# Mixers: longer waits in the planner for the delta rule's decay products, and the linear attention's copies and updates first in VectorE's order

## The chip, the cores and the metric

The kernel runs on one core of one Trainium2 chip. The metric is the device time of one execution in microseconds (us). TensorE multiplies matrices, VectorE and ScalarE work element by element and read the matmuls' results from PSUM, GpSimd does element-wise work in SBUF, and SyncE issues the transfers of weights.

## The reference, cut to what matters

Two transformer blocks over 512 tokens of width 1024, in float32. The first block's token mixer is what the change touches. It projects the normed input with w_in and runs four groups of heads: softmax attention with a forget gate ("fox", four heads), a gated delta rule in chunks of 64 ("gdn", four heads), and two gated linear attentions in chunks of 16 ("hg" and "gla", four heads each):

```python
# gated delta rule, per chunk of 64
decay = exp(where(causal, G[r] - G[s], -inf))
m     = where(strict, (kb @ k.T) * decay, 0)          # then solve (m + I) w = ..., (m + I) u = ...
a_qk  = where(causal, (q @ k.T) * decay, 0)
v_new = u - w @ state
o     = q_in @ state + a_qk @ v_new
state = state * a + k_out.T @ v_new
# gated linear attention, per chunk of 16
o     = q_in @ state + a_intra @ v
state = state * a + k_out.T @ v
```

The heads' outputs are normed, gated and projected with w_out. After that come a gated feed-forward with a short convolution, a block with a short-convolution mixer and a feed-forward, and a block with latent attention and a feed-forward. None of these is touched.

## The kernel before, in words

Everything is laid out with features on the 128 partitions and the 512 tokens along the free axis. A float32 product is made of three matmuls: each operand is split into a rounded part and a rest (xh and xl, wh and wl), ScalarE makes the rounded part (L111), VectorE the rest (L112). One tile of a dense product has eight steps of three matmuls each, and the weights of a whole tile are split in one ScalarE and one VectorE instruction.

In the mixers TensorE's order is the program's (`manual_schedule`), and `conduct` writes it. It is a planner with a clock of its own, `clk`, which only TensorE's work moves (`mm` and `tr` add an estimate for each matmul; a dense one of 512 columns counts 0.216). Three lanes of work, linear attention (PSUM tag lps), delta rule (gps) and fox (fps), each with two PSUM buffers, are Python generators. A generator issues some work and then yields the time that it expects the other engines to need for it; the planner takes it up again when its clock has passed that time, and fills in with steps of the dense products (w_in's tiles, then w_out's) until then. The constants are LA = 0.68 (about one ScalarE instruction), LV = 1.0 (one on VectorE), LP = 1.5 (one on GpSimd). Where the yielded time is too short, TensorE reaches an instruction whose operand or buffer isn't ready, and waits.

The order on VectorE, ScalarE and GpSimd is made when the program is built, by a scheduler with its own estimate of when each instruction becomes ready: among those ready it takes the earliest in the program, and those issued under `high_priority` before all others. On the chip each engine then runs its instructions in that order. Before the change, `high_priority` stood in the delta rule: at gy (L1138), gx (L1143), gxt (L1146), gvt (L1191) and the state gst (L1212).

`gdn(p)` runs for two pairs of heads. It transposes k and q into tokens, squares them (ScalarE), copies k's tokens to gko (ScalarE, L1062), forms the norms, and then yields 0.0. For each head j of the pair it issues the decay products (an identity matmul of a mask, shown as gps<-mixb,identb, and four of gps<-mixc,gg), and ScalarE's exponentials gmt (L1088); yields; the k·q product, weighted on VectorE into gat (L1031); yields LV; the k·k product, weighted into gmt (L1031), with gmr, u and gxt; and yields LV. After that comes the inverse by doubling, six levels with gy, gx and gxt, and the recurrence over four blocks of 128 tokens.

`la` runs three times in its lane: hg0, gla, hg1. For each of seven block sizes it issues the product of lw and lbd, four blocks of tokens wide (or two for gla), and the part of the result that belongs to this level is copied into the attention matrix lat: on ScalarE at the first level (L1366), on VectorE with `copy_predicated` under a mask at the other six (L1368). Then the next but one level's lw and lbd are made. At the end four blocks of tokens are run through, with a state lst that VectorE updates: a copy for the first block (L1406), state times decay plus product for the second and third (L1408). Outputs are normed in `finish`, which transposes them back into a PSUM buffer of the same lane and multiplies them into a gate (L1022).

Of the kernel before, what the change touches and what calls it, by code (L numbers as in the profile page):

```python
# [15 lines left out]
ALU = mybir.AluOpType  # L16
# [629 lines left out]
LA, LV, LP = 0.68, 1.0, 1.5  # L646
# [17 lines left out]
class Mix(Mla):  # L664
# [371 lines left out]
    def gdn(self, p):  # L1036
        nc = self.nc
# [16 lines left out]
        for i, y in enumerate((k, q)):  # L1054
# [4 lines left out]
                out=ss[:, 8 - 8 * i : 16 - 8 * i], in_=sq.rearrange("p (a d) -> p a d", d=64), axis=AX.X, op=ALU.add  # L1059
# [11 lines left out]
        nc.vector.tensor_tensor(out=kof, in0=kof, in1=ik, op=ALU.mult)  # L1071
        nk = self.s1(8, "gnk", 2)
        nc.vector.tensor_tensor(out=nk, in0=ss[:, 8:16], in1=rr[:, 8:16], op=ALU.mult)
        yield 0.0
        MT, MR, AT, X, XT = [], [], [], [], []
        for j in range(2):
            rows = slice(64 * j, 64 * j + 64)
            gp = self.pst()
            self.mm(c4(gp), self.identb, bc(self.negt), stop=False)
            for c in range(4):  # L1080
                col = 4 * c + 2 * p + j
                self.mm(
                    gp[:, c * 128 : c * 128 + 128], self.g[:, col : col + 1].to_broadcast([128, 128]), self.triu,
                    start=False, stop=(c == 3),
                )
            e = self.b("gmt", bufs=2)
            for c in range(4):
                nc.scalar.activation(  # L1088
                    out=e[:, c * 128 : c * 128 + 128], in_=gp[:, c * 128 : c * 128 + 128], func=ACTF.Exp,
                    bias=bias[:, 2 * c + j : 2 * c + j + 1],  # L1090
                )
            yield Y_GDN / (1 + j)
            kp = self.pst()
            for c in range(4):
                cs = slice(c * 128, c * 128 + 128)
                self.mm(kp[:, cs], k[rows, cs], q[rows, cs])
            at = self.b("gat", bufs=2)
            self.weighted(at, kp, ik, j, e)
            yield LV
            kp = self.pst()  # L1100
            for c in range(4):
                cs = slice(c * 128, c * 128 + 128)
                self.mm(kp[:, cs], k[rows, cs], k[rows, cs])
            mt = e
            self.weighted(mt, kp, ik, j, e)
            mr = self.b("gmr", F32R, bufs=2)
            nc.scalar.activation(out=mr, in_=mt, func=ACTF.Copy)
            xt = self.b("gxt", F32R, bufs=2)
            t1 = self.t(tag="s")
            nc.vector.tensor_tensor(out=c4(t1), in0=c4(mt), in1=bc(self.nm1), op=ALU.mult)  # L1110
            nc.vector.tensor_tensor(out=c4(xt), in0=c4(t1), in1=bc(self.ident), op=ALU.add)
            MT.append(mt), MR.append(mr), AT.append(at), XT.append(xt)
            yield LV
        nc.gpsimd.tensor_tensor(out=d4(ke), in0=d4(ko), in1=b64(eG), op=ALU.mult)
        nc.gpsimd.tensor_tensor(out=d4(ko), in0=d4(ko), in1=b64(h2(kof)), op=ALU.mult)
        tp = self.to_tokens(v)
# [8 lines left out]
        for lv in range(6):  # L1125
            b = 2 << lv
# [12 lines left out]
            for j in range(2):  # L1139
                yield LV  # L1140
                pp = self.mm4(XT[j], Y[j], up)
# [3 lines left out]
                with self.tc.high_priority():  # L1145
                    nc.vector.scalar_tensor_tensor(  # L1146
                        out=lo(XT[j]), in0=lo(pt), scalar=self.grow[:, lv : lv + 1], in1=lo(f1(XT[j])),
                        op0=ALU.mult, op1=ALU.add,
# [31 lines left out]
        st = None  # L1180
        yield LA
        for c in range(4):
# [3 lines left out]
            else:  # L1186
# [3 lines left out]
                with self.tc.high_priority():  # L1190
# [5 lines left out]
                    out=h64(os_[:, cs]), in0=h64(qp[:, 0:128]),  # L1196
                    in1=eG[:, c].unsqueeze(2).to_broadcast([128, 2, 64]), op=ALU.mult,
                )
                yield 0.5
            if c < 3:  # L1200
                kp = self.pst()
# [120 lines left out]
    def la(self, q, k, f, vts, nh, es, pair, gates, g, scale):  # L1322
# [30 lines left out]
        for lv, b in enumerate(LEVELS):  # L1353
            w, bd = ws[lv]
            per = 512 // (nh * 64)
            for c0 in range(0, 4, per):
                yield wait
                wait = LV
                pp = self.pst().rearrange("p (c h r) -> p c h r", c=per, h=nh)
                for c in range(per):  # L1360
                    cs = slice((c0 + c) * 128, (c0 + c) * 128 + 128)
                    self.mm(pp[:, c], w[:, cs], bd[:, c0 + c])
                for h in range(nh):
                    at = c4(AT[h])[:, c0 : c0 + per]
                    if lv == 0:
                        nc.scalar.activation(out=at[0:64, :, 64:128], in_=pp[0:64, :, h], func=ACTF.Copy)  # L1366
                    else:
                        nc.vector.copy_predicated(  # L1368
                            out=at.rearrange("p c (n j) -> p c n j", j=2 * b)[:, :, :, b:],
                            mask=self.lmask[:, lv - 1].rearrange("p (n j) -> p n j", j=b).unsqueeze(1)  # L1370
                            .to_broadcast([128, per, 64 // b, b]),
                            data=pp[:, :, h].rearrange("p c (n j) -> p c n j", j=b),
                        )
            if lv + 2 < len(LEVELS):
                ws.append(self.la_level(lv + 2, q, k, g128, g16, es, nh))
                wait = LV + LP
# [17 lines left out]
        for c in range(4):  # L1394
            cs = slice(c * 128, c * 128 + 128)
            yield LV
            if c < 3:
                kp = self.pst()
                for i in range(nh // 2):
                    self.mm(kp[:, i * 128 : i * 128 + 128], ko[:, cs], vts[i][:, cs])  # L1400
                new = self.ph.tile([128, 256], F32, tag="lst", name="lst", bufs=2)
                nc.gpsimd.memset(new, 0.0)
                for h in range(nh):
                    rs, vs = slice(h * dk, h * dk + dk), slice(h * 64, h * 64 + 64)
                    if st is None:
                        nc.vector.tensor_copy(out=new[rs, vs], in_=kp[rs, vs])  # L1406
                    else:
                        nc.vector.scalar_tensor_tensor(  # L1408
                            out=new[rs, vs], in0=st[rs, vs], scalar=ea[rs, c : c + 1],
                            in1=kp[rs, vs], op0=ALU.mult, op1=ALU.add,  # L1410
                        )
            op = self.pst()
            for i in range(nh // 2):
                ob = op[:, i * 128 : i * 128 + 128]
                if st is not None:
                    self.mm(ob, qi[:, cs], st[:, i * 128 : i * 128 + 128], stop=False)
                for j in range(2):
                    hs = slice(c * 128 + j * 64, c * 128 + j * 64 + 64)
                    self.mm(
                        ob[:, j * 64 : j * 64 + 64], AT[2 * i + j][:, cs], vts[i][:, hs],  # L1420
                        start=(c == 0), stop=(c == 0 or j == 1),
                    )
            for i in range(nh // 2):
                nc.scalar.activation(out=os_[i][:, cs], in_=op[:, i * 128 : i * 128 + 128], func=ACTF.Copy)
            if c < 3:
                st = new
# [268 lines left out]
```

## Time and profile before

| | |
|---|---|
| median of 3 runs | 1861.06 us (1860.66 to 1865.96) |
| profiled execution | 1856.94 us |
| its span | 1855.1 us, granted clock 0.994 |
| TensorE busy | 1817.0 us (98%) |
| VectorE busy | 1055.4 us (57%) |
| ScalarE busy | 737.9 us (40%) |
| GpSimd busy | 193.8 us (10%) |

The profile is of one execution. The span goes from its first to its last instruction, and some 1.8 us of the execution lie around it. Matmuls overlap, so a busy TensorE isn't one at its peak, but a hole in it is time in which it did nothing. The granted clock is 1.00 at 2.4 GHz and 0.50 at 1.2 GHz. The engines are named PE (TensorE), PEld (its weight loads), DVE (VectorE), ACT (ScalarE), POOL (GpSimd) and SP (SyncE).

### The profile page before, as it was taken

Reading aid. Unit: us, or ns where it says so; the run is one execution under the profiler, and the core shown is the slowest. Engines: PE = TensorE matmul, PEld = TensorE weight load, DVE = VectorE, ACT = ScalarE, POOL = GpSimd, SP = SyncE. Lnnn points to the kernel's source line nnn. Section 1 sums busy time; section 2 is a strip of 40 time slices with the busy share of each in tenths; the row PEclk is TensorE's granted clock in tenths of the full one; section 3 lists DMA queues with packets and bytes.
Section 4 is the critical chain, followed back from the end, with each engine's and each line's share of the span. In section 5 each row is a group of like instructions: output and inputs, shape, how many; then the busy total and the mean of one; then the engine's idle time right before and its main releaser. Section 6 shows DMA issues by size and latency. Waiting matters only on the chain.

```text
span 1855.1 us, 22054 instructions
## 1 busy us (share of the span) xinstructions
PE 1817.0 (98%) x8609; PEld 1501.1 (81%) x8609; DVE 1055.4 (57%) x1627; ACT 737.9 (40%) x1138; POOL 193.8 (10%) x225
## 2 busy tenths in 40 slices
PE   8999999999999999999999999999999999999997
PEld 6787788778888888888888888888787888888886
DVE  7885976767777633555564444333876454444323
ACT  6544535454444422322342323323577333232322
POOL 1511402210000001111200000010011200000001
PEclk9999999999999999999999999999999999999999
DMA  5111110322223233232323232333212232323332
GB/s 168 57 42 40 48 38 30 120 95 96 99 95 102 86 96 103 91 102 92 102 96 103 91 102 92 94 97 105 64 57 75 79 103 91 102 91 99 94 94 77
DMA packets 53223, 162.61 MB, mean 88 GB/s; under 512 B 6528, under 2 KB 13184, under 8 KB 53120
## 3 DMA queue, kind: packets, MB, share of 16 engines
q1 hardware_dynamic: 52992, 161.21, 27.2%
q8 instruction: 67, 1.10, 0.2%
q14 instruction: 36, 0.29, 0.1%
q10 hardware_dynamic: 128, 0.01, 0.0%
HBM read 157.78 MB, written 2.10 MB: 86 GB/s over the span
## 4 chain that ended last, share of the span: by engine, by line
PE 86%; DVE 8%; ACT 4%; issue 1%; POOL 1%; DMA 0%; SPq 0%; DVEq 0%; POOLq 0%; ACTq 0%
PE mm L125 24%; PE mm L127 24%; PE mm L126 24%; PE mm L705 6%; PE gps L705 3%; PE lps L705 2%; PE fps L705 1%; DVE lbd L1317 1%; ACT wh L111 1%; DVE wl L112 1%; DVE lat L1368 1%; PE ps L577 0%; DVE ptl L112 0%; PE ps L165 0%; DVE nm L580 0%
## 5 line engine op out<-in xcount | busy, mean ns | idle before, releaser
L111 ACT ACTIVATE wh<-raw 128x1024 fp32r<-128x1024 f32 (+3 forms) x308 | 308.6, 1003 | 765.3 <-PE mm L126 459.4
L125 PE MATMUL mm<-xh,wh 128*128 128x512 f32 x1336 | 521.8, 391 | 0.4 <-ACT xh L173 0.4
L126 PE MATMUL mm<-xl,wh 128*128 128x512 f32 x1336 | 520.7, 390 | 0.5 <-DVE xl L174 0.5
L127 PE MATMUL mm<-xh,wl 128*128 128x512 f32 x1336 | 519.9, 389 | 0.0
L112 DVE TENSOR_TENSOR wl<-raw,wh 128x1024 fp32r<-128x1024 f32 (+3 forms) x300 | 362.1, 1207 | 226.0 <-ACT wh L111 222.9
L126 PEld LDWEIGHTS mm<-xl,wh 128*128 128x128 f32 x1336 | 250.8, 188 | 54.6 <-DVE xl L174 1.4
L125 PEld LDWEIGHTS mm<-xh,wh 128*128 128x128 f32 x1336 | 250.8, 188 | 53.7 <-issue 1.0
L127 PEld LDWEIGHTS mm<-xh,wl 128*128 128x128 f32 x1336 | 250.8, 188 | 52.1 <-issue 0.2
L125 PE MATMUL mm<-hidh,wh 128*128 128x512 f32 (+1 forms) x614 | 236.7, 386 | 0.0
L127 PE MATMUL mm<-hidh,wl 128*128 128x512 f32 (+1 forms) x614 | 235.3, 384 | 0.0
L126 PE MATMUL mm<-hidl,wh 128*128 128x512 f32 (+1 forms) x614 | 233.8, 381 | 0.0
L127 PEld LDWEIGHTS mm<-hidh,wl 128*128 128x128 f32 x614 | 115.4, 188 | 24.2
L705 PE MATMUL mm<-xh,wh 128*128 128x512 f32 x291 | 127.9, 439 | 6.8 <-ACT xh L173 6.0
L126 PEld LDWEIGHTS mm<-hidl,wh 128*128 128x128 f32 x614 | 115.4, 188 | 23.6
L125 PEld LDWEIGHTS mm<-hidh,wh 128*128 128x128 f32 x614 | 115.5, 188 | 21.9 <-ACT wh L111 0.2
L705 PE MATMUL mm<-xh,wl 128*128 128x512 f32 x291 | 116.1, 399 | 0.8 <-DVE wl L112 0.8
L705 PE MATMUL mm<-xl,wh 128*128 128x512 f32 x291 | 115.9, 398 | 0.4 <-DVE xl L112 0.4
L278 DVE TENSOR_TENSOR u<-mm,rb 128x512 f32<-128x512 f32 x44 | 30.4, 691 | 140.9 <-PE mm L127 140.9
L158 POOL TENSOR_TENSOR z<-z,sq 128x512 f32<-128x512 f32 x31 | 50.3, 1624 | 557.3 <-ACT sq L156 519.6
L274 DVE TENSOR_TENSOR u<-mm,rb 128x512 f32<-128x512 f32 x44 | 30.4, 691 | 90.9 <-PE mm L127 90.8
L111 ACT ACTIVATE hidh<-s 128x512 fp32r<-128x512 f32 x66 | 41.8, 633 | 88.3 <-DVE s L255 57.5
L705 PEld LDWEIGHTS mm<-xh,wh 128*128 128x128 f32 x291 | 56.5, 194 | 19.1 <-ACT xh L173 6.7
(434 smaller groups left out, 2087.3 us busy)
## 6 DMA issues: line engine op xcount, KB each, us to landing
raw<-in_w_a_dram SPq DMA_DIRECT2D x52, 512.0 KB, 3.3
raw<-in_w_b_dram SPq DMA_DIRECT2D x52, 512.0 KB, 3.3
raw<-in_w_up_dram SPq DMA_DIRECT2D x44, 512.0 KB, 3.3
raw<-in_w_in_dram SPq DMA_DIRECT2D x28, 512.0 KB, 3.3
raw<-in_conv_w_in_dram SPq DMA_DIRECT2D x24, 512.0 KB, 3.3
raw<-in_w_down_dram SPq DMA_DIRECT2D x16, 448.0 KB, 3.3
raw<-in_w_a_dram SPq DMA_DIRECT2D x16, 448.0 KB, 3.3
raw<-in_w_b_dram SPq DMA_DIRECT2D x16, 448.0 KB, 3.3
```

Source lines behind the costliest of these rows:

```text
L111: nc.scalar.activation(out=h, in_=src, func=ACTF.Copy)
L112: (eng or nc.vector).tensor_tensor(out=l, in0=src, in1=h.bitcast(F32), op=ALU.subtract)
L125: nc.tensor.matmul(out=ps, lhsT=h, rhs=xh, start=(k == 0), stop=False)
L126: nc.tensor.matmul(out=ps, lhsT=h, rhs=xl, start=False, stop=False)
L127: nc.tensor.matmul(out=ps, lhsT=l, rhs=xh, start=False, stop=(k == kt - 1))
L158: eng.tensor_tensor(out=acc, in0=acc, in1=sq, op=ALU.add)
L274: nc.vector.tensor_tensor(out=g, in0=ps, in1=r, op=ALU.mult)
L278: nc.vector.tensor_tensor(out=g, in0=ps, in1=r, op=ALU.mult)
L705: self.nc.tensor.matmul(out=out, lhsT=lhsT, rhs=rhs, start=start, stop=stop)
L1317: nc.vector.tensor_tensor(out=bd[rows, :, h].rearrange("p c (n j) -> p c n j", j=b), in0=c4(q)[rows], in1=c4(d)[rows], op=ALU.mult)
L1368: nc.vector.copy_predicated(out=at.rearrange("p c (n j) -> p c n j", j=2 * b)[:, :, :, b:], mask=self.lmask[:, lv - 1].rearrange("p (n j) ...
```

## The change

Two yields in `gdn` are longer: the one ahead of the decay products goes from 0.0 to 2 × LA = 1.36, and the one behind the first head's k·k product from LV = 1.0 to 2.5 × LV = 2.5 (behind the second head's it stays LV). In `la`, the masked copies and the state updates are issued under `high_priority`. No instruction is added or removed.

```diff
@@ gdn @@
         nk = self.s1(8, "gnk", 2)
         nc.vector.tensor_tensor(out=nk, in0=ss[:, 8:16], in1=rr[:, 8:16], op=ALU.mult)
-        yield 0.0
+        yield 2 * LA
         MT, MR, AT, X, XT = [], [], [], [], []
...
             MT.append(mt), MR.append(mr), AT.append(at), XT.append(xt)
-            yield LV
+            yield LV if j else 2.5 * LV
         nc.gpsimd.tensor_tensor(out=d4(ke), in0=d4(ko), in1=b64(eG), op=ALU.mult)
@@ la @@
                     else:
-                        nc.vector.copy_predicated(
+                        with self.tc.high_priority():
+                            nc.vector.copy_predicated(
...
                 nc.gpsimd.memset(new, 0.0)
-                for h in range(nh):
+                with self.tc.high_priority():
+                    for h in range(nh):
...
```

## Rows read from the trace of the kernel before

**Rows 1.** Windows: busy us (x) of PE, PEld, DVE, ACT, POOL; clock; DMA share; GB/s.
```profile
40.00:405.00 365.00, 351.29 (x2012) 293.27 (x2011) 272.36 (x570) 176.13 (x344) 91.71 (x91) 0.98 0.18 57
405.00:1855.00 1450.00, 1433.58 (x6478) 1183.69 (x6477) 749.57 (x986) 536.72 (x750) 96.02 (x114) 1.00 0.29 93
```

**Rows 2.** Waits of TensorE, 40 to 405 us: total us, times, longest us.
```profile
PE lps L705 <- DVE gate L1022: 2.0, 1, 2.0
PE lps L705 <- DVE lat L1368: 1.7, 1, 1.7
PE gps L705 <- DVE gat L1031: 1.5, 1, 1.5
PE lps L705 <- DVE lst L1408: 1.3, 1, 1.3
PE gps L705 <- ACT gko L1062: 1.3, 2, 1.1
PE mm L705 <- ACT wh L111: 0.9, 1, 0.9
PE lps L705 <- DVE lst L1406: 0.6, 1, 0.6
```

**Rows 3.** Windows inside the mixers, same columns as rows 1.
```profile
62.00:100.00 38.00, 36.47 (x229) 31.24 (x229) 33.64 (x65) 13.24 (x30) 20.91 (x18) 1.00 0.17 56
...
232.00:235.00 3.00, 2.95 (x12) 2.65 (x12) 2.14 (x7) 0.00 (x0) 0.00 (x0) 0.58 0.33 128
235.00:238.50 3.50, 3.50 (x11) 2.85 (x11) 1.10 (x4) 0.00 (x0) 0.02 (x1) 0.50 0.02 5
...
345.00:348.70 3.70, 3.24 (x12) 2.99 (x13) 3.65 (x7) 1.57 (x2) 0.00 (x0) 0.54 0.24 87
```

**Rows 4.** Timeline of TensorE: start us, us, instruction, idle before and releaser.
```profile
49.62 0.50 PE L705 MATMUL mm<-xh,wl 128*128 128x512 f32 x1 [0.53 <-DVE wl L112]
...
52.06 0.38 PE L705 MATMUL gps<-mixb,identb 128*128 128x512 bf16 x1 [1.07 <-ACT gko L1062]
...
64.70 0.38 PE L705 MATMUL gps<-mixb,identb 128*128 128x512 bf16 x1 [1.53 <-DVE gat L1031]
```

**Rows 5.** Timeline of VectorE, 61 to 65 us.
```profile
61.94 1.67 DVE L112 TENSOR_TENSOR wl<-raw,wh 128x1024 fp32r<-128x1024 f32 x1 [0.81 <-ACT wh L111]
63.53 1.11 DVE L1031 SCALAR_TENSOR_TENSOR gat<-gps,gik,gmt 128x128 f32<-128x128 f32 x4
```

**Rows 6.** One line's instructions: ns min/median/max, first and last start us.
```profile
L1368 DVE COPY_PREDICATED lat<-lmask,lps x72: 282/426/787, 85.6 to 350.9; 128x128 f32<-128x128 uint8 x48, 128x256 f32<-128x256 uint8 x24
...
L1408 DVE SCALAR_TENSOR_TENSOR lst<-lst,lea,lps x16: 263/276/291, 117.6 to 362.5; 64x64 f32<-64x64 f32 x8, 32x64 f32<-32x64 f32 x8
...
L1224 DVE TENSOR_TENSOR gx<-gx,gps x6: 286/288/289, 155.2 to 319.3; 128x128 f32<-128x128 f32 x6
```

**Rows 7.** Timeline around two state updates.
```profile
113.78 0.38 PE L705 MATMUL lps<-lv,lko 128*128 128x128 f32 x2
...
116.88 0.47 DVE L1406 COPY lst<-lps 64x64 f32<-64x64 f32 x2
...
259.63 0.29 DVE L1408 SCALAR_TENSOR_TENSOR lst<-lst,lea,lps 32x64 f32<-32x64 f32 x1
```

**Rows 8.** Timeline, 338 to 345 us.
```profile
338.79 1.05 PE L705 MATMUL lps<-lbd,lw 128*128 128x128 f32 x8
...
344.57 0.74 DVE L1368 COPY_PREDICATED lat<-lmask,lps 128x256 f32<-128x256 uint8 x2
```

**Rows 9.** Timeline of VectorE, 231 to 235 us.
```profile
231.27 0.72 DVE L1022 SCALAR_TENSOR_TENSOR gate<-lps,fg,gate 128x512 f32<-128x512 f32 x1
231.91 1.00 DVE L1368 COPY_PREDICATED lat<-lmask,lps 128x128 f32<-128x128 uint8 x3
233.77 0.72 DVE L1368 COPY_PREDICATED lat<-lmask,lps 128x128 f32<-128x128 uint8 x2 [0.86 <-PE lps L705]
234.46 0.42 DVE L1143 TENSOR_TENSOR gx<-gx,gps 128x256 fp32r<-128x256 f32 x1
```

More of the change, by code (lines that the diff above doesn't have):

```diff
@@ L1367, in la @@
                     else:
-                        nc.vector.copy_predicated(
[L1369 to L1373, printed above, removed]
+                        with self.tc.high_priority():
+                            nc.vector.copy_predicated(
+                                out=at.rearrange("p c (n j) -> p c n j", j=2 * b)[:, :, :, b:],
+                                mask=self.lmask[:, lv - 1].rearrange("p (n j) -> p n j", j=b).unsqueeze(1)
+                                .to_broadcast([128, per, 64 // b, b]),
+                                data=pp[:, :, h].rearrange("p c (n j) -> p c n j", j=b),
+                            )
             if lv + 2 < len(LEVELS):
@@ L1402, in la @@
                 nc.gpsimd.memset(new, 0.0)
-                for h in range(nh):
[L1404 to L1411, printed above, removed]
+                with self.tc.high_priority():
+                    for h in range(nh):
+                        rs, vs = slice(h * dk, h * dk + dk), slice(h * 64, h * 64 + 64)
+                        if st is None:
+                            nc.vector.tensor_copy(out=new[rs, vs], in_=kp[rs, vs])
+                        else:
+                            nc.vector.scalar_tensor_tensor(
+                                out=new[rs, vs], in0=st[rs, vs], scalar=ea[rs, c : c + 1],
+                                in1=kp[rs, vs], op0=ALU.mult, op1=ALU.add,
+                            )
             op = self.pst()
```

## The prediction

> **What bounds the kernel now.** I read the busy time of the engines by stage first [rows 1]. From 405 us to the end TensorE is busy 1433.6 of 1450 us, and nothing that the change touches runs there. The mixers lie between 40 and 405 us, with TensorE busy 351.3 of 365 us at a mean granted clock of 0.98. TensorE's own order is written by hand, so a matmul that isn't ready holds up everything behind it; the stage costs TensorE's work, plus its holes, plus what is lost at the lower clock. 365 − 351.3 = 13.7 us of holes is the most that better waits could give back there. Elsewhere TensorE does 6478 matmuls in 1450 us, 0.224 us each, so a step of three dense matmuls lasts about 0.67 us.
>
> The list of what TensorE waited for [rows 2] names the causes: VectorE's gate L1022 2.0 us, lat L1368 1.7, gat L1031 1.5, lst L1408 1.3 and L1406 0.6, and ScalarE's gko L1062 1.3 in two pieces. Four of these six lines belong to places that the change edits; gate L1022 doesn't, and gko and gat are reached by the waits.
>
> The windows by clock [rows 3] show what a hole can cost behind it. After the 2.0 us hole that ends at 232 us the granted clock was 0.58 until 235 and 0.50, which is 1.2 GHz, until 238.5: (1 − 0.58) × 3 + 0.5 × 3.5 = 3.0 us. From 345 to 348.7 it was 0.54: 0.46 × 3.7 = 1.7 us. From 62 to 100 us, with one hole of 38 − 36.47 = 1.53 us, it stayed at 1.00. So I count clock only where a low clock stands in a row.
>
> **Part 1, the wait before the decay products** (0 to 2 × LA = 1.36). The planner counts 0.216 for a dense matmul, 0.648 for a step, so 1.36 lets it put up to three steps (3 × 0.67 = 2.0 us) ahead of the first decay product of each delta-rule pair. There TensorE stood idle 1.07 us, until gko had freed the PSUM buffer, and the product began at 52.06 [rows 4]. Are steps ready? The step at 49.62 had waited for wl of a tile whose eight steps share one wl, and seven were left, so yes. Gain 1.07 us, and the other piece of gko's 1.3, 0.2 us, in the second pair: 1.3. The steps aren't new work: they are taken from a later place. The products with w_out run on after the last lane has ended, so dense work isn't what the stage's end is short of; the cost is nothing as long as that holds, and the steps' 2.0 us if it doesn't. Bounds 0.9 to 1.3.
>
> **Part 2, the wait before the second head's decay product** (LV = 1.0 to 2.5 × LV). Two or three more steps, 1.3 to 2.0 us. In the first pair the product at 64.70 came 1.53 us late [rows 4]: its buffer was held by the first product until gat (63.53, 1.11 for four) had read it, and gat stood behind wl (61.94, 1.67) [rows 5]. Steps are ready there too: the list's largest wait for a weight split is 0.9 us, once [rows 2], and it belongs to the tile of the step at 49.62. Gain 1.3 to 1.5; I take 1.4. In the second pair no such hole is in the list: nothing gained, nothing lost. What is delayed is the delta rule itself, by about 3.4 us in each pair. Behind it waits its own chain, and then the output products that need its heads; the last linear-attention head starts state updates until 362.5 us, the delta rule its last sums at 319.3 [rows 6], so even 7 us later the delta rule isn't the last.
>
> **Part 3, the state updates first on VectorE.** 16 updates with a median of 276 ns [rows 6], and the first copies beside them. The copy at 116.88 answers a product at 113.78; other work of VectorE ran ahead of it, and TensorE waited 0.6 us [rows 2, 7]. At 259.63 the last of four updates ran, behind other work again, and TensorE waited 1.3 us. Put first, each group would run right behind its product: gain 1.9, the two lines of the list. The work moved back is at most four updates of 0.28 us, 1.1 us, on a root or a weight split that has slack in most places. Bounds 1.0 to 1.9; I take 1.7.
>
> **Part 4, the masked copies first.** 72 copies, median 426 ns [rows 6], in 24 groups, 12 of two and 12 of four (128x256 and 128x128). Nothing is added, only order. Two places pay. At 344.57 two copies free a PSUM buffer whose product began at 338.79 [rows 8]; splits and a gate ran ahead of them; TensorE waited 1.7 us and then lost 1.7 us to the clock, 3.4 together. With the copies first, the splits xl that the dense steps need come 0.74 us later, and TensorE waits for those instead, perhaps twice: I take 3.4 − 2 × 0.74 = 1.9, bounds 0 and 3.4. At 231.27 the other way: gate L1022 holds the second of the two buffers, and three copies (231.91, 1.00) now behind it would go ahead of it [rows 9]. The 2.0 us hole then grows by up to 1.0; I take a loss of 0.5. Its cause, transposes issued before the gate that reads them can run, isn't touched by the change.
>
> **Sum.** 1.3 + 1.4 + 1.7 + 1.9 − 0.5 = 5.8 us less; with all good bounds 1.3 + 1.5 + 1.9 + 3.4 = 8.1, with all bad ones 0.9 + 1.3 + 1.0 + 0 − 1.0 = 2.2. Against the profiled execution (1856.94, its span 1855.10 and 1.84 around it) that is 1851.1. The three timed runs have their median 4.1 higher, at 1861.06, and the forecast is made for such a median: 1861.06 − 5.8 = 1855.3. About 0.3%, 5.6 us, is what a measurement of this kernel tells from no change, so the forecast stands right at that edge.
>
> **Rival 1: later waits take it back (no change).** VectorE is busy 272.4 of 365 us in the stage [rows 1], but 33.6 of 38 us from 62 to 100 [rows 3]. If TensorE comes 2.7 us earlier into such a stretch, what it asks VectorE for isn't earlier, and the 2.7 us of parts 1 and 2 come back as other waits. Moreover five or six steps moved shift every later meeting of the three lanes; holes that now happen to be closed may open. For it: the holes of the list are spread over all lanes, so each reshuffle draws new ones. Against it: from 65 to 100 us TensorE had no hole, with VectorE that full. Then 5.8 − 2.7 = 3.1 less at best, and about 1858; the outer end is no gain, 1861.
>
> **Rival 2: copies block VectorE (slower).** VectorE runs its instructions in the order given. At 233.77 copies waited 0.86 us for their product while a gx that the delta rule needed stood behind [rows 9]. The Trainium skill, page TensorE: Matmul & The Clock Gate, the table at its head, gives VectorE a strict first-in, first-out queue, while TensorE's can reorder in part; by that rule a copy placed too early stops all behind it, and the 0.86 us row agrees. The mechanism: a group ahead of gy, gx or gxt delays the delta rule by two copies, 2 × 0.43 = 0.86 us, and TensorE, in its fixed order, waits. It decides from 5.8 / 0.86, about 7 of the 24 groups. If 15 collide without slack, 15 × 0.86 = 12.9 − 5.8 = 7 us slower, 1868, and low-clock stretches of 1.7 to 3.0 us could join. Against it: the planner leaves two waits of 1.0 between a delta product and the one that needs it, and copies already interleave with that chain where no hole is listed.
>
> **Rival 3: the edit doesn't take effect.** Being first only counts among instructions ready at the same time in the scheduler's own timing. If that timing has the copies and updates ready late, parts 3 and 4 give nothing: 2.7 us less, about 1858.4, no measurable change.
>
> **How the numbers follow.** The sum's case, 2 to 8 us less: 0.42. It straddles the edge of 5.6; its middle, 5.8, lies just beyond, so 0.26 of it is faster and 0.16 within. A luckier reshuffle that also closes other holes, such as the 2.0 us and the 3.0 us of clock around 232 us: 0.16, 1846 to 1852. Rival 1: 0.20. Rival 3: 0.07. Rival 2: 0.15, of which 0.14 beyond the edge. Faster is 0.26 + 0.16 = 0.42, same 0.16 + 0.20 + 0.07 + 0.01 = 0.44, slower 0.14. The likeliest case is the sum, 1855.3, its own range 1853 to 1859. The range for all reaches to the luckier reshuffle and to rival 2's price: 1847 to 1867 leaves out about 0.05 below and 0.12 above.
>
> **What would show it.** Right: no wait for gko before the first decay product and none for gat before the third buffer; lst L1406 and L1408 gone from TensorE's list; the hole at 345 us shorter, with a granted clock near 1.00 behind it; gate L1022 still there. Stage busy time of TensorE unchanged, and the stage some 6 us shorter. Wrong: new entries for gx, gxt, gy, or xl in TensorE's list that add up to more than what went; a longer wait for gate L1022; more windows at 0.5; or the copies in the same places as now.

## The result and the profile after

The changed kernel took 1888.34 us (median of 6 runs, 1875.19 to 1892.71), the kernel before 1860.03 us (6 runs, 1854.81 to 1865.96): ratio 1.0165 [1.0144, 1.0186]. That is 28 us slower where the sum said 5.8 us faster, and outside the range. In all ratios here, executions that ran far longer at a lower clock are left out (one of the experiment e1_waits, 1902.92 us at 0.975, and one of e16_push, 2340.83 us at 0.726, the only one of that kernel with a trace, so that this trace isn't used); the medians are over all runs. The profiled execution took 1887.35 us, its span 1885.6, at a mean granted clock of 0.985 (before: 0.994).

First the windows of the changed kernel, to be read against [rows 1, 3] (busy us of PE, PEld, DVE, ACT and POOL, then the granted clock):

```profile
40.00:425.00 385.00, 358.35 (x1974) 299.82 (x1973) 266.35 (x558) 172.26 (x336) 86.20 (x90) 0.94 0.16 52
425.00:1885.00 1460.00, 1443.72 (x6518) 1190.87 (x6516) 757.21 (x998) 542.57 (x759) 96.23 (x115) 1.00 0.29 93
62.00:100.00 38.00, 34.18 (x198) 29.41 (x197) 29.89 (x58) 13.51 (x29) 19.47 (x18) 0.91 0.12 42
130.00:133.50 3.50, 1.02 (x8) 0.88 (x8) 1.11 (x6) 2.77 (x7) 0.10 (x1) 0.98 0.00 0
133.50:140.00 6.50, 6.50 (x24) 5.82 (x25) 2.46 (x7) 0.88 (x3) 0.00 (x0) 0.50 0.00 0
140.00:160.00 20.00, 20.00 (x71) 16.90 (x70) 6.29 (x13) 3.69 (x9) 2.54 (x2) 0.50 0.08 26
```

Everything happened in the mixers. Their end, taken as the first matmul of the next part (L125), came at 425.19 us, before at 393.88: 31.3 us later. From 40 us to that end TensorE's holes (length less busy time) are 26.7 us, and were 12.7; the low clock (the sum over 5 us windows of one less the granted clock, times the length) cost 23.9, and 6.8 before. 14.0 + 17.1 = 31.1 us, so the two account for all of it. Without them the end is at 374.6 in this trace and 374.4 in that of before: no work was added. The largest piece of clock is in the last three windows: from 133.5 to 160 us TensorE was busy all the time and had 0.50, 1.2 GHz.

What TensorE waited for, 40 to 425 us (total us, times, longest), against [rows 2]:

```profile
PE fps L705 <- ACT fpt L1484: 6.5, 2, 4.0
PE lps L705 <- ACT lv L1275: 3.8, 1, 3.8
PE fps L712 <- ACT fp L1472: 2.9, 1, 2.9
PE gps L712 <- DVE u L1007: 2.4, 1, 2.4
PE mm L705 <- ACT xh L111: 2.3, 2, 1.5
PE lps L705 <- DVE lat L1369: 1.9, 1, 1.9
```

gko, gat, both lst lines and gate L1022 have gone from the list; lat has stayed. Beside it stand waits that the list of before didn't have, most of them for ScalarE. None of fpt, lv and fp is on a line that the change edits.

The first of them in TensorE's timeline (start, length, instruction, idle time before and its releaser), against [rows 4]:

```profile
53.12 0.39 PE L705 MATMUL gps<-mixb,identb 128*128 128x512 bf16 x1
...
60.20 0.66 PE L712 MATMUL lps<-mlac,lv 128*128 128x128 f32 x4
...
62.48 1.05 PE L705 MATMUL lps<-lq,lk 64*128 64x128 f32 x8
...
68.94 0.79 PE L705 MATMUL lps<-lq,lk 64*128 64x128 f32 x2 [3.82 <-ACT lv L1275]
```

And what ScalarE did meanwhile:

```profile
64.34 0.62 ACT L1380 ACTIVATE lqi<-lg 128x512 f32<-128x512 f32 x1
67.69 0.42 ACT L1307 ACTIVATE s<-s 128x256 f32<-128x256 f32 x1 [2.73 <-POOL s L1306]
68.01 0.40 ACT L1308 ACTIVATE s<-s 128x256 f32<-128x256 f32 x1
68.31 0.58 ACT L1275 ACTIVATE lv<-lps 128x512 f32<-128x512 f32 x1
```

The first decay product starts at 53.12 with no wait: Part 1's hole is closed. Then the planner, with a longer wait to fill, put not only dense steps ahead of the second decay product but also both q·k products of the linear attention (lps<-lq,lk; in the trace of before they start at 65.90 and 68.56, behind that decay product at 64.70, here at 62.48 and 68.94, ahead of it at 70.95). That is how `conduct` works: a lane that is due goes before a dense step, which the account of the planner ahead of the prediction left out. There are two lps buffers; the first q·k product (62.48) has one, the transposes of lv (60.20) the other until ScalarE copies it. In ScalarE's order that copy stands behind exponentials (L1307 and L1308) that wait for GpSimd (2.73 us), so it runs at 68.31, and TensorE stands from 65.1 to 68.94. In the trace of before, ScalarE read lv at 66.94 and the second q·k product came at 68.56, with no hole.

By the Trainium skill (page "TensorE: Matmul & The Clock Gate", the table at its head) ScalarE's queue is strictly first in, first out; the trace agrees, since lv's transposes had ended 7 us before the copy ran, behind the waiting exponentials.

The hole for fp has another kind of work in front. ScalarE again:

```profile
127.33 1.28 ACT L261 ACT_TABLE_LOAD   x1
129.93 0.63 ACT L261 ACTIVATE gk<-gk 128x512 f32<-128x512 f32 x1 [1.31 <-DVE gk L228]
130.57 1.28 ACT L264 ACT_TABLE_LOAD   x1
131.87 0.21 ACT L882 ACTIVATE finr<-fm 128x8 f32<-128x8 f32 x1
131.98 0.35 ACT L1472 ACTIVATE fp<-fps,nm 128x128 f32<-128x128 f32 x1
```

A silu brings two table loads of 1.28 us with it, and here a wait for VectorE in between. From 127.33 to 131.85 ScalarE did nothing but this, and the fox lane's exponential fp came 2.9 us late. The 4.0 us for fpt at 283 us is the same meeting, with a silu of two tiles (278.69 to 282.43).

The lines of [rows 6] in the changed kernel (ns least, median, most; first and last start):

```profile
L1369 DVE COPY_PREDICATED lat<-lmask,lps x72: 280/430/785, 88.0 to 378.3; 128x128 f32<-128x128 uint8 x48, 128x256 f32<-128x256 uint8 x24
...
L1410 DVE SCALAR_TENSOR_TENSOR lst<-lst,lea,lps x16: 268/276/290, 119.6 to 392.3; 64x64 f32<-64x64 f32 x8, 32x64 f32<-32x64 f32 x8
...
L1224 DVE TENSOR_TENSOR gx<-gx,gps x6: 286/289/289, 177.7 to 373.1; 128x128 f32<-128x128 f32 x6
```

None of the three became dearer. The delta rule's last sum moved from 319.3 to 373.1 us, the last state update from 362.5 to 392.3: the delta rule is later by far more than the 3.4 us a pair that I counted, and still isn't the last.

### The profile page after: what moved, and what is told of

It reads as the page before. It is cut to its first block, busy times and chain, and to the rows that moved or that the text cites. A ratio compares the mean times of both kernels' runs of the same rounds, so it can differ in the third digit from the quotient of the medians.

```text
span 1885.6 us, 22069 instructions
## 1 busy us (share of the span) xinstructions
PE 1832.3 (97%) x8609; PEld 1513.2 (80%) x8609; DVE 1056.6 (56%) x1627; ACT 739.5 (39%) x1138; POOL 189.4 (10%) x225
## 4 chain that ended last, share of the span: by engine, by line
PE 86%; DVE 7%; ACT 4%; issue 1%; POOL 1%; DMA 0%; DVEq 0%; SPq 0%; ACTq 0%; POOLq 0%
PE mm L125 24%; PE mm L127 24%; PE mm L126 24%; PE mm L705 8%; PE gps L705 3%; PE lps L705 2%; PE fps L705 1%; ACT wh L111 1%; DVE wl L112 1%; DVE lat L1369 1%; DVE lbd L1317 0%; POOL s L1306 0%; PE ps L577 0%; DVE ptl L112 0%; ACT L264 0%
## 5 line engine op out<-in xcount | busy, mean ns | idle before, releaser
L125 PE MATMUL mm<-xh,wh 128*128 128x512 f32 x1336 | 521.8, 391 | 0.2 <-ACT xh L173 0.2
L112 DVE TENSOR_TENSOR wl<-raw,wh 128x1024 fp32r<-128x1024 f32 (+3 forms) x300 | 366.6, 1222 | 225.1 <-ACT wh L111 221.8
L125 PEld LDWEIGHTS mm<-xh,wh 128*128 128x128 f32 x1336 | 250.8, 188 | 53.3 <-issue 1.0
L125 PE MATMUL mm<-hidh,wh 128*128 128x512 f32 (+1 forms) x614 | 236.7, 386 | 0.0
L125 PEld LDWEIGHTS mm<-hidh,wh 128*128 128x128 f32 x614 | 115.5, 188 | 21.8 <-ACT wh L111 0.2
```

Source lines behind the costliest of these rows:

```text
L112: (eng or nc.vector).tensor_tensor(out=l, in0=src, in1=h.bitcast(F32), op=ALU.subtract)
L125: nc.tensor.matmul(out=ps, lhsT=h, rhs=xh, start=(k == 0), stop=False)
```

## The experiments

My theory after the comparison of the traces (A): the two longer waits make the lanes meet at new places in TensorE's fixed order, and holes open there. The rival (B): copies and updates that go first hold up VectorE. One table for all kernels; in the ratio each stands against runs of the kernel before that were taken with it. "Time × clock" is the median over the runs of time times mean granted clock, so roughly what the runs would have taken without low clock, an estimate (the clock is given to 0.001, so it is good to about 1 us). End, holes and clock lost are of the profiled execution, worked out as above.

| kernel | median us | ratio to before | time × clock | mixers' end | holes | clock lost |
|---|---|---|---|---|---|---|
| before | 1855 to 1860 | | 1845.7 | 393.9 | 12.7 | 6.8 |
| after | 1888.34 | 1.0165 [1.0144, 1.0186] | 1858.2 | 425.2 | 26.7 | 23.9 |
| e1_waits | 1875.73 | 1.0104 [1.0080, 1.0128] | 1858.8 | 411.8 | 25.6 | 12.0 |
| e2_first | 1853.06 | 0.9982 [0.9967, 0.9997] | 1847.5 | 390.0 | 14.8 | 0.0 |
| e3_wait1 | 1861.37 | 1.0040 [1.0015, 1.0065] | 1846.9 | 394.1 | 14.6 | 5.1 |
| e4_wait2 | 1865.64 | 1.0046 [1.0029, 1.0063] | 1855.2 | 399.1 | 19.3 | 3.4 |
| e11_pair0 | 1896.67 | 1.0197 [1.0161, 1.0234] | 1857.8 | 433.5 | 25.4 | 34.2 |
| e12_pair1 | 1863.48 | 1.0041 [1.0027, 1.0055] | 1851.5 | 401.1 | 17.5 | 8.6 |
| e5_copies | 1856.58 | 1.0006 [0.9989, 1.0023] | 1850.0 | 394.6 | 15.7 | 3.4 |
| e6_states | 1852.20 | 0.9984 [0.9974, 0.9994] | 1844.0 | 388.8 | 12.7 | 1.8 |
| e9_gko_gat_first | 1853.34 | 0.9990 [0.9981, 1.0000] | 1848.7 | 390.6 | 13.9 | 1.7 |
| e10_lv_vector | 1871.58 | 1.0096 [1.0066, 1.0126] | 1856.6 | 408.5 | 24.0 | 10.3 |
| e13_fpt_vector | 1880.77 | 1.0140 [1.0092, 1.0189] | 1855.4 | 421.2 | 23.6 | 23.9 |
| e14_lv_fpt_vector | 1880.83 | 1.0121 [1.0075, 1.0166] | 1853.4 | 404.8 | 21.1 | 8.5 |
| e16_push | 1877.54 | 1.0121 [1.0106, 1.0137] | 1857.9 | | | |
| e17_gko5 | 1871.14 | 1.0091 [1.0077, 1.0105] | 1850.9 | 406.9 | 21.4 | 15.4 |
| e18_small | 1861.54 | 1.0036 [1.0023, 1.0048] | 1848.3 | 398.8 | 14.2 | 10.2 |
| e19_small_states | 1860.70 | 1.0029 [1.0018, 1.0041] | 1845.3 | 397.2 | 13.3 | 10.3 |
| e20_small_lv | 1855.95 | 1.0005 [0.9990, 1.0020] | 1847.1 | 399.7 | 14.3 | 10.2 |
| e21_small_lv_states | 1854.28 | 0.9991 [0.9976, 1.0005] | 1845.1 | 394.0 | 11.4 | 8.5 |

In every row with a trace but e17's (370.1), end less holes less clock lost is 373.6 to 376.4. So the question for each kernel is only which holes it has, and what clock they brought.

**Which half carries the loss.** e1_waits has the two yields alone, e2_first the two priorities alone.

```diff
# e1_waits
-        yield 0.0
+        yield 2 * LA
...
-            yield LV
+            yield LV if j else 2.5 * LV
# e2_first: copy_predicated (L1368) and lst's updates under high_priority
```

> Only the two longer yields; VectorE's choice rule as before. Theory A (the moved steps make the three lanes meet at new places in TensorE's fixed order): nearly all of the loss is here, 15 to 32 us slower than before, with the 3.8 us wait for lv near 65 us and the 2.9 us wait for fp near 130 us again. Theory B (copies and updates placed first hold up the rest of VectorE's queue): at most 3 us slower, or 2 to 3 us faster as the holes at the two decay products go.

> Only the copies and the state updates first; both yields as before, so that TensorE's written order is that of before. Theory A: within 6 us of before. Theory B: 15 to 30 us slower. If the two parts only hurt together, both this and the run with the yields alone lie within 6 us.

The waits carry it: A holds, B falls. TensorE's order is the same in e1_waits and after, and so, within a microsecond, is the time × clock; after's further 0.6% is clock (its runs lie at 0.981 to 0.991, those of e1 in the ratio at 0.991 to 0.992).

**Which wait, and which pair.** e3_wait1 and e4_wait2 have one yield each, for both pairs; e11_pair0 and e12_pair1 both yields, for one pair.

```diff
# e3_wait1
-        yield 0.0
+        yield 2 * LA
# e4_wait2
-            yield LV
+            yield LV if j else 2.5 * LV
# e11_pair0 (e12_pair1: the other pair)
+        yield 0.0 if p else 2 * LA
...
+            yield LV if j or p else 2.5 * LV
```

> Only the first yield, 0.0 to 2 x LA. Theory A in general: a shift of three steps is enough to lose, 5 us or more slower. A narrower form of A, that the place of the second q-k product of the linear attention ahead of the second decay product makes the loss: this one doesn't move it, so 0 to 4 us faster, the 1.1 us hole for gko gone. Theory B: 1 us faster.

> Only the second yield, LV to 2.5 x LV. Narrower form of A: 10 to 30 us slower, with a wait for lv of 2 us or more ahead of the second q-k product of the linear attention, and a stretch at the low clock behind it. Theory B: 1 to 2 us faster.

> Both longer waits, but for the first pair of heads of the delta rule alone (p = 0); the second pair, copies and updates as before. TensorE's order differs from before from the first decay product on (near 52 us). Both waits for both pairs cost 1.0%, 20 us. If the loss is what the lanes meet later, after the first pair has been moved, nearly all of it is here: 14 to 20 us above before, with the holes for lv (3.8 us) and fp (2.9 us). If each pair's own delay costs (the delta rule comes late at its end), each pair carries about half, 8 to 12 us.

> Both longer waits for the second pair alone (p = 1). TensorE's order is that of before up to some 230 us, so the holes for lv at 68 us and fp at 131 us can't be there. If the loss is a matter of where the lanes meet, this order is a draw of its own: between 3 us less and 10 us more, and not the rest of the sum (20 us less the first pair's). If each pair's own delay costs, it is 8 to 12 us more.

Each wait alone loses about 0.4%, together 1.04%. The narrower reading, that only the q·k product moved by the second yield matters, expected a gain from e3 and from e4 a far larger loss with a hole of 2 us or more for lv; that hole is 0.7 us in e4, so this reading falls. In e3 a hole for lv (1.7 us) and one for fp (1.2) take back the 1.1 us for gko; by time × clock it loses only 1.3 us, the rest is clock (its runs lie at 0.985 to 0.995). The first pair alone has as much time × clock as both pairs (1857.8 against 1858.8); the second pair alone loses 6 us, so they don't add. The order of TensorE's instructions in the traces fits this: with one of the waits (e3, e4) the order parts from that of before in the first pair and is the same again from some 103 us on (in e4 until the second pair, near 210 us), while with both waits in the first pair (after, e1, e11) it doesn't come back. e4 and e12 have the same order from 103 us on, and the same holes in the second pair. One new hole of e12 (ScalarE's order, and the product that waited for it):

```profile
289.89 1.28 ACT L261 ACT_TABLE_LOAD   x1
291.18 0.63 ACT L261 ACTIVATE lq<-lq 128x512 f32<-128x512 f32 x1
291.72 0.61 ACT L261 ACTIVATE gate<-gate 128x512 f32<-128x512 f32 x1
292.35 1.28 ACT L264 ACT_TABLE_LOAD   x1
293.65 0.31 ACT L1492 ACTIVATE rq<-fps,sm 128x64 f32<-128x64 f32 x1
```

```profile
294.01 1.37 PE L705 MATMUL fps<-fk,fq 65*128 65x384 f32 x2 [2.58 <-ACT rq L1492]
```

The silu and its two table loads again, 3.7 us in all, with another fox instruction caught behind it.

**The priorities apart, and the two targeted holes by priority.** e5_copies and e6_states have one priority each; e9_gko_gat_first is e2 with the copy gko and the weighting gat under `high_priority` too.

```diff
# e5_copies: copy_predicated alone; e6_states: lst's updates alone
# e9_gko_gat_first, on top of e2_first
+                with self.tc.high_priority():
                     nc.scalar.activation(out=ko, in_=tp, func=ACTF.Copy)
...
+            with self.tc.high_priority():
                 self.weighted(at, kp, ik, j, e)
```

> Only the masked copies first, waits and state updates as before. My sum's Part 4 put this at 1.9 - 0.5 = 1.4 us less (bounds: 1.0 slower to 3.4 less), so a ratio near 0.999. Theory A (all the loss comes from the moved steps of TensorE's order) expects 0 to 4 us less, with the lat hole at 344.57 shortened and TensorE's order as before. A rest of Theory B (copies block VectorE, 0.86 us a group) would show 3 or more us slower here, and be hidden in the run with both priorities by what the updates gain.

> Only the state updates first. Part 3 put this at 1.7 us less (bounds 1.0 to 1.9): both lst entries (1.3 and 0.6 us) leave TensorE's list of waits. If the priorities do nothing because the updates are already where they can be (the third rival), the list keeps lst at 1.3 or more and the time is within 0.1% of before.

> Waits as before, the copies and updates first, and beside them ScalarE's copy gko and VectorE's gat and first gmt of each pair first in their engines' order. It goes for the same two holes as the waits (1.07 and 1.53 us) without moving a step of TensorE. If those holes are only a matter of order on ScalarE and VectorE, both go: 2.0 to 2.6 us less than with the copies and updates alone (which was 0.2% below before), so some 0.3 to 0.35% below before. If gko and gat are late for their inputs and not for their place, the holes stay and the time is that of the copies and updates alone.

The updates first gain 0.16%: 2.7 us in the medians, 1.6 by time × clock. But in the profiled execution the holes are as long as before (12.7 us). The two lst holes at 117.39 and 259.97 us closed as foreseen (0.63 and 1.31), and two others opened (TensorE's timeline of e6_states):

```profile
119.86 0.46 PE L705 MATMUL lps<-lst,lqi 128*128 128x128 f32 x2 [0.83 <-DVE lst L1409]
...
290.85 0.88 PE L705 MATMUL fps<-fv,fpt 128*128 128x64 f32 x6 [1.05 <-ACT fpt L1483]
```

In front of this fpt stands a silu again, from 286.55 to 290.29 us. The 5 us by which the mixers end earlier in this trace are all clock: the holes for gate (1.99) and lat (1.75) are still there, but behind the gate's the low clock cost 1.75 us in place of 3.4, and the low stretches from 290 and from 345 us, 1.7 us each in before, aren't there. So the updates first are worth having, but that fewer holes are the reason isn't shown.

The copies first gain nothing; by time × clock they cost 4 us, which a higher clock covers. TensorE's timeline in e5_copies:

```profile
222.78 0.66 PE L712 MATMUL gps<-mlac,gxt 128*128 128x128 f32 x4 [1.42 <-DVE gmt L1031]
...
225.81 0.63 PE L712 MATMUL gps<-mlac,gxt 128*128 128x128 f32 x4 [0.81 <-DVE gxt L1111]
...
235.05 1.10 PE L705 MATMUL lps<-lbd,lw 128*128 128x256 f32 x4 [1.15 <-DVE lat L1369]
...
346.08 1.13 PE L705 MATMUL lps<-lbd,lw 128*128 128x128 f32 x8 [1.12 <-DVE lat L1369]
...
351.00 0.50 PE L705 MATMUL mm<-xl,wh 128*128 128x512 f32 x1 [1.27 <-DVE xl L112]
```

The hole for lat at 345 us shrank from 1.73 to 1.12 us, and behind it comes a wait of 1.27 us for an xl: before, two copies ran behind this xl (348.51 on VectorE), now they run ahead of it (349.13). Where the gate's 1.99 us stood there are three waits of the delta rule and the linear attention, 1.42 + 0.81 + 1.15 = 3.4 us: gmt starts 3 us later on VectorE than before (221.61 against 218.53), and copies now run there in fours between the delta rule's instructions (210.61, 212.64 and 217.51).

In e9 the holes for gko (1.07) and gat (1.53) stayed as they were, because the edit moved neither of them there. VectorE's order round gat is that of before:

```profile
61.66 1.67 DVE L112 TENSOR_TENSOR wl<-raw,wh 128x1024 fp32r<-128x1024 f32 x1 [0.81 <-ACT wh L111]
63.26 1.11 DVE L1031 SCALAR_TENSOR_TENSOR gat<-gps,gik,gmt 128x128 f32<-128x128 f32 x4
```

gat's product ran from 57.77 to 58.93, its other operands were there by 57.7, and VectorE even stood idle for 0.81 us ahead of that wl; gat still came behind it, and gko behind the square u (L1057) as before. So whether an earlier place would close these two holes isn't shown. (The first gmt, which the expectation names, isn't in the edit.)

**Closing the new holes.** e10_lv_vector is the whole change with lv (L1275) copied by VectorE in place of ScalarE, first in its order; e13_fpt_vector the same with fpt (L1484); e14_lv_fpt_vector has both.

```diff
# e10_lv_vector
-        self.nc.scalar.activation(out=vt, in_=self.to_tokens(vt), func=ACTF.Copy)
+        tv = self.to_tokens(vt)
+        with self.tc.high_priority():
+            self.nc.vector.tensor_copy(out=vt, in_=tv)
# e13_fpt_vector
-            nc.scalar.activation(out=pt[:, :n], in_=tp[:, :n], func=ACTF.Copy)
+            with self.tc.high_priority():
+                nc.vector.tensor_copy(out=pt[:, :n], in_=tp[:, :n])
```

> The whole change, and beside it the copy lv of the linear attention's two heads pairs (L1275) made by VectorE, first in its order, in place of ScalarE, where it stood behind level exponentials that wait for GpSimd. TensorE's order is that of the changed kernel. Theory A says that the 3.8 us hole at 65 to 70 us opens because the moved product needs the PSUM buffer that lv frees, and that the place of lv on ScalarE makes it late: then the hole falls to under 1.5 us, the granted clock stays near 1.00 from 69 to 75 us, and the mixers end 4 to 7 us earlier than with the change (425.2), if the later holes stay as they are. If the hole comes from something else (the product's inputs, or work before it), it stays above 3 us. The other holes of the change (fp, fpt, xh) are not touched, so the kernel stays 15 or more us above before.

> The whole change, and the forgetting attention's copy fpt (L1484) made by VectorE, first in its order, in place of ScalarE, where it stood behind a silu with its two table loads (3.7 us). TensorE's order is that of the changed kernel. If that queue is the cause, fpt's 6.5 us of holes (4.0 and 2.5) go, and the clock lost behind them (1.7 and 3.4 us): the mixers end 8 to 12 us earlier than 425.2, if what lies before stays as it is, the 27 us at 1.2 GHz with it. If TensorE's order itself is too early for fpt (its exponential late), the holes stay above 4 us in sum.

> The whole change, with both lv and fpt copied by VectorE first in its order. With lv alone the mixers ended at 408.5 (holes 24.0, clock 10.3 us). If the two repairs add, fpt's 6.5 us and some 5 us of clock go as well: an end at 396 to 400, and a time 0 to 8 us above before. A time at or below before would mean that the longer waits are harmless once two copies leave ScalarE; an end above 405 that the holes move on to other waits when these are closed.

With lv on VectorE the product no longer waits long (TensorE's timeline and windows of e10_lv_vector):

```profile
65.36 1.16 PE L705 MATMUL lps<-lq,lk 64*128 64x128 f32 x8 [0.77 <-DVE lv L1277]
...
126.70 0.47 PE L712 MATMUL fps<-mlac,fp 128*128 128x128 f32 x1 [2.93 <-ACT fp L1474]
```

```profile
65.00:70.00 5.00, 4.64 (x28) 4.06 (x29) 5.00 (x13) 2.74 (x9) 3.63 (x5) 1.00 0.00 0
...
127.00:130.00 3.00, 3.00 (x13) 2.63 (x13) 2.02 (x6) 0.84 (x3) 0.00 (x0) 0.50 0.00 0
130.00:133.00 3.00, 3.00 (x10) 2.42 (x10) 0.38 (x2) 0.31 (x1) 0.00 (x0) 0.50 0.00 0
133.00:138.00 5.00, 5.00 (x34) 4.42 (x35) 3.19 (x8) 2.15 (x5) 0.00 (x0) 0.99 0.00 0
```

So the copy's place on ScalarE was the cause of that hole. But holes over the mixers fell by 2.7 us and not by 3.8, and the other 14 us by which this trace is shorter are clock: the hole for fp is as long as in after (2.93 and 2.92), and 0.50 lasted some 6 us behind it here, 26.5 there. With fpt on VectorE its 6.5 us are gone, but gx (2.1), fp (3.8 in place of 2.9) and gmr (1.5 in place of 1.0) take half of it. With both, time × clock is 1853.4, still 8 us above before. The repairs don't restore what the order of before had; the time of e14 (four runs from 1867.9 to 1888.8) went with their clock, 0.993 to 0.981.

**Holes in the old order, other orders, smaller waits.** e17_gko5 leaves TensorE's order as it was and makes gko late; e16_push puts the same dense work ahead but moves all lanes' due times along; e18_small halves both waits; e19_small_states is e18 with the updates first.

```diff
# e17_gko5
+                for _ in range(5):
                     nc.scalar.activation(out=ko, in_=tp, func=ACTF.Copy)
# e16_push: in conduct, push being 2 * LA or 1.5 * LV at the two places
+                for s in live:
+                    s.at = max(s.at, self.clk) + self.push
# e18_small
-        yield 0.0
+        yield LA
...
-            yield LV
+            yield LV if j else 1.5 * LV
```

> Before, with ScalarE's copy gko made five times over in each pair of the delta rule (same data, four of them for nothing), so that the holes for gko grow by up to some 4 x 0.6 = 2.4 us and what stood between, in TensorE's order of before. If a hole costs its length and the low clock behind it, and holes elsewhere stay, the mixers end 3 to 10 us later, and the sum 375 + holes + clock loss holds. If a late gko shifts the later meetings as the moved steps do, more holes open elsewhere: over 10 us. If slack behind the hole takes it back: under 2 us.

> Waits, copies and updates as before, but the planner puts the same dense work ahead: at the first decay product it moves the due time of all lanes back by 1.36, at the second by 1.5, and so not the delta rule's alone. TensorE's order still parts from that of before for the rest of the mixers, in other places than with the longer waits. If the loss with the waits came from the delta rule being late against the other lanes, this costs little: within 4 us of before. If it comes from any order in which the lanes meet anew, it is slower by 5 to 30 us, with holes in other places.

> Both waits half as long (0.68 and 1.5). The planner then puts two dense steps ahead of the first decay product and one or two ahead of the second, and TensorE's order is that of before again from some 90 us on. My Parts 1 and 2 at this size: the gko hole (1.07) and the gat hole (1.53) close, 2 to 2.6 us less, nothing else changes. If even a moved q-k product ahead of the second decay product is enough for the lv hole (1.7 to 3.8 us), it is 0 to 5 us more than before.

> The half-long waits and the state updates first. The updates alone were 0.16% (3 us) below before. If the small move gives its 2 to 2.6 us and nothing is lost later, the two add to 4 to 6 us less, 0.25 to 0.3% below before; if the small move opens new holes, it is no better than the updates alone.

e17 shows that holes cost their length and more in the old order too. The first gko hole was to grow from 1.07 by 2.4 us and by what stood between; it became 5.26, and two others came up behind it (TensorE's timeline):

```profile
55.87 0.59 PE L705 MATMUL gps<-mixb,identb 128*128 128x512 bf16 x1 [5.26 <-ACT gko L1063]
...
69.45 1.11 PE L712 MATMUL lps<-mlac,lv 128*128 128x128 f32 x4 [2.44 <-DVE lv L901]
...
74.66 0.59 PE L705 MATMUL gps<-mixb,identb 128*128 128x512 bf16 x1 [2.81 <-DVE gat L1031]
```

With 8.7 us more of holes and 8.6 more of clock, the mixers ended 13.0 us later. (The sum overstates by some 4 us, in the main because part of the low clock lay over idle time: 0.32 × 4.39 us of it from 50 to 55 us and 0.5 × 2.81 from 70 to 75 are 2.8.) e16 is 1.2% slower too: moving the other lanes along doesn't keep the old meetings.

e18 is the cleanest picture. TensorE's order departs from that of before only from 52 to some 107 us (up to 101 in before's time); both targeted holes close, and one opens (timeline and windows of e18_small):

```profile
63.77 0.39 PE L705 MATMUL gps<-mixb,identb 128*128 128x512 bf16 x1
...
68.61 1.16 PE L705 MATMUL lps<-lq,lk 64*128 64x128 f32 x8 [2.86 <-ACT lv L1275]
```

```profile
65.00:68.00 3.00, 0.75 (x4) 0.27 (x2) 2.97 (x7) 1.37 (x5) 3.00 (x4) 1.00 0.04 16
...
70.00:75.00 5.00, 5.00 (x16) 3.77 (x15) 2.04 (x8) 2.18 (x7) 3.40 (x3) 0.53 0.00 0
75.00:80.00 5.00, 5.00 (x16) 3.64 (x16) 3.02 (x6) 2.32 (x3) 0.00 (x0) 0.50 0.26 75
```

1.07 + 1.53 = 2.6 us of holes went, 2.86 for lv and 1.2 for fp came, and behind lv's hole 0.47 × 5 + 0.5 × 5 = 4.9 us of clock. That is the prediction's Parts 1 and 2 in miniature, and it loses 0.36%. The updates first recover 0.07% of it.

**The small waits with lv repaired.** e20_small_lv and e21_small_lv_states are e18 and e19 with the edit of e10.

> The half-long waits, and the copy lv of the linear attention's head pairs made by VectorE, first in its order, in place of ScalarE. TensorE's order is that of the half-long waits alone. If the hole of 2.9 us for lv, with the low clock behind it, is all that made the half-long waits lose, it falls below 1 us, the clock from 70 to 80 us is 1.00, and the time is 2 to 5 us below before. If the loss moves elsewhere again (the copy of 0.6 us on VectorE delays gat, lat or wl, or the two table loads find other work), it is within 2 us of before or above.

> The same, and the state updates first, which alone gave 3 us. If the parts add, 5 to 8 us below before, 0.3 to 0.4%: the prediction's Parts 1 to 3 then hold with this repair. If not, no better than the updates alone (0.16% below).

The hole for lv is gone and the clock from 65 to 75 us is 1.00, but gmt 1.5 and fpt 1.1 open, so that the holes (14.3) are as long as in e18. 0.31 of e18's 0.36% comes back, no gain over before. Neither beats the updates alone: e6_states, 0.16% below before, has the lowest time here, though the intervals of e6, e2, e9 and e21 overlap.

## Why the prediction was wrong, point by point

**The step that failed** is the price of the longer waits, which Parts 1 and 2 put at nothing. Part 2 says "What is delayed is the delta rule itself", with the sentence behind it that even 7 us later the delta rule isn't the last; Part 1 says "the cost is nothing as long as that holds". I looked for cover at the end of the lanes and of the dense work, where there was enough, and not at the next few instructions of the other lanes. Both conditions even held in the changed kernel (the delta rule still ends before the linear attention, 373.1 against 392.3 us, and dense steps run on from the last lane's matmul at 402.61 us to the end at 425.19), so they were the wrong conditions. The planner fills the longer wait with whatever is due, not with dense steps alone, and a piece that comes earlier can meet a buffer whose reader on ScalarE hasn't moved, as lv shows. Priced at nothing, the two waits measured 13 us by time × clock (e1), those of the first pair alone 12 (e11).

**The local gains were real.** The holes for gko (1.07) and gat (1.53) closed in after and in e18, at the sizes foreseen. But they didn't shorten any kernel: with lv repaired, e20 has 14.3 us of holes, before 12.7. In e21 the holes are 11.4 us, 1.3 less than in before and in e6, and still its time isn't below e6's.

**Rival 1 had the mechanism,** down to "holes that now happen to be closed may open", with 0.20, but I gave it "the outer end is no gain, 1861". Nothing in the rows supported that bound. Seven orders of TensorE other than the old one were tried (that of after and e1; e3, e4, e11, e12, e16, e18); all are slower, by 0.36 to 2.0%; only the order of e18, with lv moved to VectorE as well, is level with before (e20, e21). They aren't independent draws: all put work ahead of the same two products, and e3, e4, e12 and e11 share long stretches with others of them. So they don't say how an average order would fare; the "luckier reshuffle", at 0.16, wasn't among them.

**Clock.** I counted "clock only where a low clock stands in a row", and in the sum only as something to be gained; rival 2 names it as a loss without a price. In after it made more than half of the loss, 17.1 of 31.1 us in the profiled pair.

**Part 3** has its number, 1.7 forecast and 2.7 us measured in time, 1.6 by time × clock (e6), but partly by luck. The two holes that it counted closed, 1.94 us; others of 0.83 and 1.05 us opened, so that the sum of holes stayed at 12.7, which is rival 1's "later waits take it back". The profiled execution gained by clock, which Part 3 didn't count.

**Part 4** failed: 1.4 less forecast, 1 us more measured, within the interval of none (e5). At 345 us, where I counted 1.9, the hole for lat shrank by 0.6 us and one wait for xl of 1.27 came, of the two of 0.74 that I had allowed for. At 232 us, where I allowed 0.5, the gate's hole gave way to 1.4 us more of other waits. Rival 2 is there in small (3.0 us of holes more in e5) and is not what made the kernel slower (e2).

**Rival 3** is refuted for the copies and updates: with either priority the list of waits changed. For gko and gat its mechanism is what happened in e9.

**Two readings of the rows** were off without weight in the sum. Three of the six listed lines, not four, belong to places that the change edits (lat and the two of lst). And the mixers end at 393.9 us, not at 405, so that the holes to be had there were 12.7 us, not 13.7.

## What to carry to other kernels

Where one engine's order is written out by hand and is close to full, a longer expected wait doesn't only let filler through: list what else the planner will pull into the gap, and for each piece find which engine has to free its buffer and what stands ahead of that in its queue. Long blocks in such a queue, here 3.7 us of silu with its table loads, are what a moved step can run into. And price a new hole at its length plus the low clock that has followed holes of that length in traces of the same kernel, for losses as well as for gains, and as a range: it spread widely here. Compare two schedules by their holes and by time × clock too, since a gain or loss in time alone can be clock.

## What the runs showed of the hardware

The low clock behind a hole lasts very differently. The fp hole of 2.92 us in after was followed by 26.5 us at 0.50 with TensorE busy throughout; the same hole in e10 (2.93) by about 6 us; the gate hole of 1.99 us at 232 us cost 3.4 us of clock in before and 1.75 in e6, with the same TensorE order; a hole of 4.00 us in e11_pair0 was followed by 25 us at 0.50, in these windows:

```profile
270.00:275.00 5.00, 1.05 (x7) 0.80 (x6) 3.44 (x10) 4.96 (x10) 0.00 (x0) 0.93 0.32 105
275.00:300.00 25.00, 24.94 (x86) 20.89 (x87) 9.70 (x23) 6.98 (x19) 0.00 (x0) 0.50 0.07 22
```

One program's time spreads accordingly (e14: 21 us over four runs, with the mean clock). What ends a long low stretch, and why one hole brings it and its twin doesn't, stays open.
